# A hybrid encoder layer on one core: query products behind the value evictions, the first head's attention three products later, five buffers for high halves and 51 ring tiles

## The chip, the core and the metric

The kernel runs on one core of a Trainium2 chip. Five engines work side by side, each on its own queue of instructions: TensorE (PE: matmuls and, as PEld, the loads of their weights), VectorE (DVE), ScalarE (ACT), GpSimd (POOL) and SyncE (SP, which here only issues DMAs). The metric is the device time of one execution in microseconds (us); lower is better. Before the change three runs took 2608.44, 2610.34 and 2613.16 us, so the median is 2610.34 us.

## What is computed

One encoder layer, in fp32, over 2048 prompt tokens and 64 tokens of a second sequence with a state. The input projection makes ten groups of 1024 columns. Path A is a gated convolution of width 3. Path B is a chunked recurrence with 8 heads of 128 columns: each head needs a query `q`, a forget gate `f`, a value `iv` and an output gate `zB`.

```python
h = rms_norm(x, g_pre)
proj = jnp.einsum('btd,dn->btn', h, w_in)
vA, bA, cA, zA, q, f, iv, zB, gA, gB = split_cols(proj)
fg = lb + (1.0 - lb) * jax.nn.sigmoid(f)
logf = jnp.log(fg); kk = 1.0 - fg
qq = jax.nn.silu(q) * QK_SCALE; vv = iv
...                                   # per chunk of 64 tokens, per head:
b = jnp.cumsum(logf, axis=1)
ref = b[:, (L - 1) // 2][:, None]
qe = q * jnp.exp(b - ref); ke = k * jnp.exp(ref - b)
att = jnp.where(causal, einsum('bthk,bshk->bhts', qe, ke), 0.0)
o = einsum('bhts,bshv->bthv', att, v) + einsum('bthk,bhkv->bthv', q * jnp.exp(b), S)
S_new = jnp.exp(b_last)[..., None] * S + einsum('bshk,bshv->bhkv', k * jnp.exp(b_last[:, None] - b), v)
...
yB = einsum('btc,cd->btd', rms(o) * g_onorm * jax.nn.silu(zB), w_b_out)
merged = jax.nn.sigmoid(gA) * yA + jax.nn.sigmoid(gB) * yB
x = x + rms_norm(einsum('btd,de->bte', merged, w_o), g_post)
gate = jax.nn.sigmoid(einsum('btd,de->bte', rms_norm(x, g_ple), w_ple_gate))
x = x + einsum('btp,pd->btd', p, w_ple_proj) * gate
```

## The kernel before

**Tiles and blocks.** The 2112 tokens (the 64 stand inside the prompt, at a cut) are worked in 3 blocks of 704, each in two halves of 352 columns. Every fp32 operand is split into a high part `hi` (a cast, on ACT) and a low part `lo` (a subtraction, on DVE), and a product of two operands is three matmuls: hi·hi (L363), hi·lo (L364), lo·hi (L365). A weight tile is 128x512 (256 KB): SP loads it into a `raw` buffer (L198), ACT casts it to `hi` (L188, or L218 once the low part exists), and in block 0 DVE subtracts the low part (L188) and SP stores it as `low`. In blocks 1 and 2 SP loads the stored low part back (L219), into a buffer `lo` or `s`.

**Groups of seven products.** `sgroup` (L349) computes two column groups for both halves with seven products in place of eight, from sums of weight blocks (S1 to S4, made in block 0 by DVE at L297 and stored) and sums of operands (T1 to T4). A product is 12 matmuls of 128x352 into one PSUM bank; there are 5 banks for these (`pg`) and 3 for the attention (`pa`). The products go to the banks a, c, d, b, a, c, d. ACT copies the banks of the first three (L377), DVE adds the fourth (L383), and the last three are evicted by a function `sink` that the caller gives, through `into` (L407 on ACT, L409 on DVE) and `whole` (L402). With `by_k` the first four products advance together, k by k.

**Path B of a block.** `path_b` (L1014 to L1032) goes over the heads. `head_prep` (L826) runs one group for F and Q and one for ZB and IV. After the third product of the second group its inner function `scaled` is called (as `mid`): three exponentials and a Silu on ACT (L855 to L859), then on DVE the scaled keys `ka` and `kb` (L874 to L879), the product of neighbouring chunk factors (L880, on 128x5), the scaled queries `qe` (L881) and `qx` (L882). `sink_v` (L884) evicts the values into `vt` and the gate into `z`. `head_attn` (L896) is a generator in four steps for each part of the block (one of four 128-token tiles and shorter ones): transposes and scores (L929 to L952), state updates (L958, L975), output and its mean square (L994 to L1003), the transpose back (L1008) and the gate (L1010). The steps lie in a list `hooks`; after each product one is taken from it, so that the attention of one head runs between the products of the next. For the first head of block 0 three empty entries are put ahead (L1026).

**Around it.** Each block runs gates (`gates`), path B, path A, the merge of both (block 0: `merge`, then blocks 1 and 2: `in_turn` with L496 to L498), the output projection and the last gate (L529 to L531). A tile scheduler decides the final order on each engine: it follows the order of the program and priorities (`high_priority`, `issue_after`, `behind_all`), and gives a tile that is written a slot of its pool as soon as the slot's last use lets it. On each engine instructions start in that order, so what stands behind a waiting one waits too.

**Pools that the change touches.** Tiles `r` come from a ring of `RING` slots of 708 fp32 per partition (L40). The weight pool has 5 slots for `raw`, 4 for `hi`, 4 for `lo` and 3 for `s`. POOL issues loads into `r` slots: the spilled gates and outputs (L1081), the next block's columns of x (L643), the weights for the sums of the next stage (L320).

Of the kernel before, what the change touches and what calls it, by code (L numbers as in the profile page):

```python
# [11 lines left out]
F32R = mybir.dt.float32r  # L12
# [6 lines left out]
P = 128  # L19
# [17 lines left out]
BN = 704  # L37
HN = BN // 2
NB = TOK // BN
RING = 52  # L40
HALVES = 9

LEAD = 7
# [39 lines left out]
def hybrid_step(  # L83
# [22 lines left out]
    wp = ctx.enter_context(tc.tile_pool(name="wp", bufs=4))  # L106
# [8 lines left out]
    def nm(s):  # L115
        uid[0] += 1
        return f"{s}_{uid[0]}"
# [94 lines left out]

    def split_w(raw, key=None, queue=SP):

        hi = wp.tile([P, 4, P], F32R, tag="hi", name=nm("hi"))
        if key in lows:
            lo = low_tile()
            A.copy(hi, raw)  # L218
            SP.dma_start(lo.bitcast(F32), lows[key])  # L219
            return hi, lo  # L220
        lo = wp.tile([P, 4, P], F32R, tag="lo", name=nm("lo"))
        split(raw, hi, lo)
        if key is not None:
            lows[key] = dram.tile([P, 4, P], F32, tag=f"lo{key}", name=nm("low"), bufs=1)
            queue.dma_start(lows[key], lo.bitcast(F32))
        return hi, lo
# [12 lines left out]
    last, hooks, copies, adds = [None], [], [None], [None]  # L239
# [154 lines left out]
    def half(t, h):  # L394
        return t[:, h * HN : (h + 1) * HN]
# [9 lines left out]
    def into(dst, x, y):  # L405
        if y is None:
            A.copy(dst, x)  # L407
        else:
            V.tensor_tensor(dst, x, y, ALU.add)  # L409
# [413 lines left out]
    def chunks(t):  # L823
        return t.rearrange("p (c t) -> p c t", t=CH)

    def head_prep(bl, hc, hd, first, hs):  # L826
        n, npair = bl["n"], bl["npair"]
        nch, np1 = n // CH, npair * P
        sf, qe = rt(), rt()

        def sink_f(c, h, x, y):
            if c == 0:
                A.activation(half(sf, h), whole(x, y), AF.Sigmoid)
            else:
                into(half(qe, h), x, y)

        if hs and hd == 0:
            plain_group(FF * 8, QQ * 8, hs, sink_f)
        else:
            sgroup(FF * 8 + hd, QQ * 8 + hd, hc, sink_f, first)  # L840
        lg, b, eq = rt(), rt(), rt()
        A.activation(lg, sf, AF.Ln, bias=lb[:, hd : hd + 1], scale=omlb[:, hd : hd + 1])
        A.activation(sf, sf, AF.Identity, bias=omlb[:, hd : hd + 1], scale=nomlb[:, hd : hd + 1])
        V.tensor_tensor_scan(b, keep[:, :n], lg, 0.0, ALU.mult, ALU.add)
        ref = chunks(b)[:, :, CH // 2 - 1 : CH // 2]
        V.tensor_tensor(chunks(lg), chunks(b), ref.to_broadcast([P, nch, CH]), ALU.subtract)
        qc = small.tile([P, 2, BN // CH], F32, tag="qc", name=nm("qc"))
        f, r = qc[:, 0, :nch], qc[:, 1, :nch]
        ka, kb, qx, vt, z = hf(HN + 32), rt(), rt(), rt(), rt()

        def scaled(after):


            with tc.issue_after(after):
                A.activation(r, ref.rearrange("p c o -> p (c o)"), AF.Exp)  # L855
                A.activation(eq, lg, AF.Exp)
                exps = A.activation(lg, lg, AF.Exp, scale=-1.0).ins
            with tc.issue_after(exps):
                A.activation(qe, qe, AF.Silu)  # L859
            V.tensor_tensor(f[:, 1:nch], r[:, 1:nch], chunks(eq)[:, : nch - 1, CH - 1], ALU.mult)  # L860
            V.tensor_copy(f[:, 0:1], r[:, 0:1])
            for g in bl["groups"]:
                if g["sample"]:
                    c = g["off"] // CH
                    V.tensor_copy(f[:, c : c + 1], r[:, c : c + 1])
            f1, f2 = f[:, 0 : 2 * npair : 2], f[:, 1 : 2 * npair : 2]
            ka3 = ka[:, : (nch + 1) // 2 * CH].rearrange("p (g t) -> p g t", t=CH)
            two = kb[:, : 4 * P].rearrange("p (c q t) -> p c q t", q=4, t=CH)
            rest = kb[:, 4 * P : np1].rearrange("p (g c t) -> p g c t", c=2, t=CH)[:, :, 0, :]

            def pairs(x, at):
                return x[:, : 4 * P].rearrange("p (c e h t) -> p c e h t", e=2, h=2, t=CH)[:, :, :, at, :]

            V.tensor_tensor(ka3, chunks(sf)[:, 0:nch:2, :], chunks(lg)[:, 0:nch:2, :], ALU.mult)  # L874
            V.tensor_tensor(two[:, :, 1:3, :], pairs(sf, 1), pairs(lg, 1), ALU.mult)
            V.tensor_tensor(kb[:, 4 * P :], sf[:, 4 * P :], lg[:, 4 * P :], ALU.mult)
            by = f2[:, :4].rearrange("p (c e) -> p c e", e=2).unsqueeze(3).to_broadcast([P, 2, 2, CH])
            V.tensor_tensor(two[:, :, 0:4:3, :], ka3[:, :4, :].rearrange("p (c e) t -> p c e t", e=2), by, ALU.mult)
            V.tensor_tensor(rest, ka3[:, 4:npair, :], f2[:, 4:npair].unsqueeze(2).to_broadcast([P, npair - 4, CH]), ALU.mult)  # L879
            V.tensor_tensor(f2, f2, f1, ALU.mult)  # L880
            V.scalar_tensor_tensor(qe, qe, QK_SCALE, eq, ALU.mult, ALU.mult)  # L881
            V.tensor_tensor(chunks(qx), chunks(qe), f.unsqueeze(2).to_broadcast([P, nch, CH]), ALU.mult)  # L882

        def sink_v(c, h, x, y):  # L884
            if c == 1:
                into(half(vt, h), x, y)
            else:
                A.activation(half(z, h), whole(x, y), AF.Silu)

        sgroup(ZB * 8 + hd, IV * 8 + hd, hc, sink_v, first, mid=scaled)  # L890
        return dict(eq=eq, f=f, ka=ka, kb=kb, qe=qe, qx=qx, vt=vt, z=z, last=bl["last"], carry=None)

# [120 lines left out]
    def path_b(bl, hc, first, kept, fills, hs):  # L1013


        def keep_z(hd, z):
            kept["o", hd] = spill("o", hd)
            G.dma_start(kept["o", hd], z)

        for hd in range(NH):  # L1020
            d = head_prep(bl, hc, hd, first, hs)
            if not (first and hd == 0):
                next(fills, None)
            assert not hooks
            attn = [head_attn(i, gs, d, hd) for i, gs in enumerate(bl["parts"])]
            hooks.extend([None] * 3 if first and hd == 0 else [])  # L1026
            for step in range(4):
                hooks.extend(partial(next, g) for g in attn)
                if step == 2:
                    hooks.append(None)  # L1030
            hooks.append(partial(keep_z, hd, d["z"]))
# [8 lines left out]
    def ple(bl, ph, kept, held=None, shared=False):  # L1040


        for j in range(KB):
            if held is not None:
                hi, lo = held[j]
            else:
                raw = wp.tile([P, 4, P], F32, tag="raw", name=nm("raw"), bufs=5)[:, :2, :]
                SP.dma_start(raw, w_ple[j])
                with tc.high_priority():
                    hi = wp.tile([P, 4, P], F32R, tag="hi", name=nm("hi"))[:, :2, :]  # L1050
                    lo = low_tile()[:, :2, :]
                    A.copy(hi, raw)
                    SP.dma_start(lo.bitcast(F32), lows["p", j])
            t = rt()
            for s in bl["segs"]:
                pp, c = ps_attn()[:, :HN], cols_of(s)
                for k, (xhi, xlo) in enumerate(ph):
                    T.matmul(pp, hi[:, k, :], xhi[:, c], start=k == 0, stop=False)
                    T.matmul(pp, hi[:, k, :], xlo[:, c], start=False, stop=False)
                    last[0] = T.matmul(pp, lo[:, k, :], xhi[:, c], start=False, stop=k == 1).ins  # L1060
                with tc.high_priority():
                    if shared and j < 4 and s is bl["segs"][1]:
                        V.tensor_copy(t[:, c], pp)
                    else:
                        copied = copies[0] = A.copy(t[:, c], pp).ins
            if bl["last"]:
                kept["p", j] = t
            else:
                kept["p", j] = spill("p", j)
                G.dma_start(kept["p", j], t)  # L1070
                if not shared:
                    lows["p", j] = dram.tile([P, 2, P], F32, tag=f"lop{j}", name=nm("low"), bufs=1)
                    SP.dma_start(lows["p", j], lo.bitcast(F32))
            with behind_all((copied,) if hooks else ()):
                hook()
            yield
# [299 lines left out]
    for bi, bl in enumerate(blocks):  # L1376
        first, kept = bi == 0, kepts[bi]
# [124 lines left out]
```

## Time and profile before

| | |
|---|---|
| runs | 2608.44, 2610.34, 2613.16 us (median 2610.34) |
| profiled execution | 2611.61 us, span 2609.9 us |
| granted TensorE clock | 1.000 |
| PE busy | 2588.6 us, 99% of the span, 16562 matmuls |
| PEld busy | 2572.5 us, 99% |
| DVE busy | 1667.1 us, 64% |
| ACT busy | 1538.9 us, 59% |
| POOL busy | 392.6 us, 15% |
| DMA | 745.99 MB, mean 286 GB/s |

The profiled execution is one run, 1.27 us longer than the median of the others. A row of the timeline gives the start in us, the duration in us, then engine, line, operation, output and inputs with the shape and, where the engine had been idle, for how long and what released it. Successive matmuls overlap in the records: each is shown as about 0.32 us long, and in a steady stretch one starts 0.16 us after the other, so a lost time on PE is read from the distance of starts. "x3" in a row means that it stands for three instructions.

### The profile page before, as it was taken

The page shows a single profiled execution, that of the slowest core. Times are in us where ns is not written, and L with a number is a line of the kernel's source. Part 1 is how long each engine was busy: PE and PEld are TensorE (multiplying, and loading weights), DVE is VectorE, ACT ScalarE, POOL GpSimd, SP SyncE. Part 2 cuts the span into 40 slices and gives each one's busy share as a digit, 9 for nine tenths or more (in the row PEclk, how much of TensorE's full clock was granted, in tenths as well). Part 3 has the DMA queues.
Part 4 walks back from the last instruction along what each step waited for, and adds up shares of the span by engine and source line. Part 5 has one row for each costly group of instructions (what it writes and reads, how often), then busy time and mean ns, then how long its engine had stood idle before and what let it go on. Part 6 is the DMA issues. An engine that isn't in the chain of part 4 may idle for free.

```text
span 2609.9 us, 47443 instructions
## 1 busy us (share of the span) xinstructions
PE 2588.6 (99%) x16562; PEld 2572.5 (99%) x16562; DVE 1667.1 (64%) x3232; ACT 1538.9 (59%) x2940; POOL 392.6 (15%) x722
## 2 busy tenths in 40 slices
PE   8999999999999999999999999999999999999999
PEld 8999999999999999999999999999999999999998
DVE  8778888888766555455545568553455544568756
ACT  6666665554434644677745556466667744555746
POOL 2000000200441212101112211021000101210220
PEclk9999999999999999999999999999999999999999
DMA  7687787898988997777789989599776789999977
GB/s 285 234 275 259 251 285 257 306 318 286 342 292 285 351 320 259 248 231 224 226 288 359 381 311 312 193 359 358 229 230 220 224 256 335 377 321 309 339 256 240
DMA packets 362672, 745.99 MB, mean 286 GB/s; under 512 B 44640, under 2 KB 49280, under 8 KB 362432
## 3 DMA queue, kind: packets, MB, share of 16 engines
q1 hardware_dynamic: 319680, 579.55, 65.4%
q0 software_dynamic: 42464, 163.37, 17.0%
q8 instruction: 130, 2.13, 0.3%
q14 instruction: 110, 0.90, 0.1%
q10 hardware_dynamic: 288, 0.05, 0.0%
HBM read 531.74 MB, written 211.04 MB: 285 GB/s over the span
## 4 chain that ended last, share of the span: by engine, by line
PE 89%; DMA 3%; DVE 2%; issue 2%; ACT 1%; POOL 1%; DVEq 0%; POOLq 0%; ACTq 0%; SPq 0%
PE pg L363 19%; PE pg L365 19%; PE pg L364 19%; PE pg L496 4%; PE pg L497 4%; PE pg L498 4%; PE pg L530 4%; PE pg L531 4%; PE pg L529 4%; PE pa L994 1%; PE pa L958 1%; PE pa L996 1%; PE pa L944 1%; DMA r<-w_blk 1%; DMA raw<-S 1%
## 5 line engine op out<-in xcount | busy, mean ns | idle before, releaser
L363 PE MATMUL pg<-r,hi 128*128 128x352 f32 x3304 | 1092.9, 331 | 4.6 <-DVE r L409 3.1
L364 PE MATMUL pg<-r,hi 128*128 128x352 f32 x3304 | 1067.6, 323 | 0.0
L365 PE MATMUL pg<-r,lo 128*128 128x352 f32 x2356 | 762.1, 323 | 1.2 <-DMA lo<-low 1.2
L218 ACT CAST hi<-raw 128x512 fp32r<-128x512 f32 x720 | 445.0, 620 | 499.8 <-PE pg L364 165.6
L363 PEld LDWEIGHTS pg<-r,hi 128*128 128x128 f32 x3304 | 622.2, 188 | 9.1 <-DVE r L409 3.2
L364 PEld LDWEIGHTS pg<-r,hi 128*128 128x128 f32 x3304 | 622.2, 188 | 0.0
L365 PEld LDWEIGHTS pg<-r,lo 128*128 128x128 f32 x2356 | 442.3, 188 | 1.8 <-DMA lo<-low 1.7
L365 PE MATMUL pg<-r,s 128*128 128x352 f32 x948 | 306.2, 323 | 0.1
L530 PE MATMUL pg<-r,hi 128*128 128x352 f32 x768 | 248.4, 324 | 0.0
L529 PE MATMUL pg<-r,hi 128*128 128x352 f32 x768 | 248.1, 323 | 0.0
L188 ACT CAST hi<-raw 128x512 fp32r<-128x512 f32 x218 | 134.6, 621 | 153.1 <-PE pg L364 53.5
L188 DVE TENSOR_TENSOR r<-r,r 128x352 fp32r<-128x352 f32 (+3 forms) x298 | 182.8, 637 | 62.7 <-ACT r L188 61.7
L497 PE MATMUL pg<-r,hi 128*128 128x352 f32 x672 | 217.3, 325 | 0.0
L496 PE MATMUL pg<-r,hi 128*128 128x352 f32 x672 | 213.6, 325 | 0.1
L531 PE MATMUL pg<-r,lo 128*128 128x352 f32 x656 | 211.9, 323 | 0.1
L188 ACT CAST r<-r 128x352 fp32r<-128x352 f32 (+3 forms) x298 | 162.2, 580 | 56.9 <-DVE r L1114 15.4
L188 DVE TENSOR_TENSOR lo<-raw,hi 128x512 fp32r<-128x512 f32 x218 | 149.4, 687 | 63.5 <-ACT hi L188 55.2
L365 PEld LDWEIGHTS pg<-r,s 128*128 128x128 f32 x948 | 178.4, 188 | 0.4 <-DMA s<-low 0.4
L188 ACT CAST hi<-s 128x512 fp32r<-128x512 f32 x160 | 98.5, 621 | 123.0 <-PE pg L364 105.8
L377 ACT COPY hf<-pg 128x352 f32<-128x352 f32 x354 | 157.1, 446 | 11.5 <-PE pg L365 10.9
L530 PEld LDWEIGHTS pg<-r,hi 128*128 128x128 f32 x768 | 144.3, 188 | 0.3 <-DVE r L188 0.2
L529 PEld LDWEIGHTS pg<-r,hi 128*128 128x128 f32 x768 | 144.2, 188 | 0.0
(367 smaller groups left out, 4157.0 us busy)
## 6 DMA issues: line engine op xcount, KB each, us to landing
raw<-w_blk SPq DMA_DIRECT2D x570, 256.0 KB, 4.2
lo<-low SPq DMA_DIRECT2D x411, 256.0 KB, 4.4
raw<-S SPq DMA_DIRECT2D x408, 256.0 KB, 4.4
low<-lo SPq DMA_DIRECT2D x314, 256.0 KB, 3.7
s<-low SPq DMA_DIRECT2D x309, 256.0 KB, 4.2
S<-s SPq DMA_DIRECT2D x152, 256.0 KB, 3.2
r<-w_blk POOLq DMA_DIRECT2D x64, 256.0 KB, 7.3
S<-r POOLq DMA_DIRECT2D x64, 256.0 KB, 5.8
```

The lines of the kernel that those rows point to most:

```text
L188: return A.copy(hi, src).ins, V.tensor_tensor(lo, src, hi.bitcast(F32), ALU.subtract).ins
L218: A.copy(hi, raw)
L363: add(hi[:, k, :], xhi, start=start and k == 0, stop=False)
L364: add(hi[:, k, :], xlo, start=False, stop=False)
L365: last[0] = add(lo[:, k, :], xhi, start=False, stop=k == KH - 1).ins
L377: copied = A.copy(got[n], ps[bank])
L496: add(hi[:, k, :], xhi, start=start and k == 0, stop=False)
L497: add(hi[:, k, :], xlo, start=False, stop=False)
L498: last[0] = add(lo[:, k, :], xhi, start=False, stop=k == KH - 1).ins
L529: T.matmul(ps, hi[:, k % 4, :], xhi[:, c], start=k == ks[0], stop=False)
L530: T.matmul(ps, hi[:, k % 4, :], xlo[:, c], start=False, stop=False)
L531: last[0] = T.matmul(ps, lo[:, k % 4, :], xhi[:, c], start=False, stop=k == ks[-1]).ins
```

## The change

Four edits. The product of chunk factors, `qe` and `qx` leave the function `scaled` and become a function `queries`, which is called when the second half of the values has been evicted. For the first head of block 0 six empty entries stand ahead of the attention in place of three. The tag `hi` gets 5 slots in place of 4 (each 512 fp32 per partition). The ring gets 51 slots in place of 52. No instruction is added or left out.

```diff
-RING = 52
+RING = 51
...
     def split_w(raw, key=None, queue=SP):
-        hi = wp.tile([P, 4, P], F32R, tag="hi", name=nm("hi"))
+        hi = wp.tile([P, 4, P], F32R, tag="hi", name=nm("hi"), bufs=5)
...
             V.tensor_tensor(rest, ka3[:, 4:npair, :], f2[:, 4:npair].unsqueeze(2).to_broadcast([P, npair - 4, CH]), ALU.mult)
+
+        def queries():
+            f1, f2 = f[:, 0 : 2 * npair : 2], f[:, 1 : 2 * npair : 2]
             V.tensor_tensor(f2, f2, f1, ALU.mult)
             V.scalar_tensor_tensor(qe, qe, QK_SCALE, eq, ALU.mult, ALU.mult)
             V.tensor_tensor(chunks(qx), chunks(qe), f.unsqueeze(2).to_broadcast([P, nch, CH]), ALU.mult)
...
         def sink_v(c, h, x, y):
             if c == 1:
                 into(half(vt, h), x, y)
+                if h == 1:
+                    queries()
...
-            hooks.extend([None] * 3 if first and hd == 0 else [])
+            hooks.extend([None] * 6 if first and hd == 0 else [])
```

Line numbers behind the edit are larger by 3 (L880 becomes L883) and, from `sink_v` on, by 5 (L1001 becomes L1006). The order on the engines moves at these places.

On DVE, in the third head of block 0 (the other heads of block 0 from the third on read alike): `r_1802` is `qe`, `r_2061` is `qx`, `r_2062` is `vt`, `pg_2155` the bank of the sixth product. Before:

```order
L880 TENSOR_TENSOR qc_2058<-qc_2058 128x5
L881 SCALAR_TENSOR_TENSOR r_1802<-r_1802,r_2053 128x704
L188 TENSOR_TENSOR lo_2310<-s_2305,hi_2309 128x512
L297 TENSOR_TENSOR s_2337<-raw_2287,s_2315 128x512
L297 TENSOR_TENSOR s_2470<-raw_2456,raw_2458 128x512
L188 TENSOR_TENSOR lo_2320<-s_2315,hi_2319 128x512
L882 TENSOR_TENSOR r_2061<-r_1802,qc_2058 128x704
L297 TENSOR_TENSOR s_2480<-raw_2458,raw_2460 128x512
L188 TENSOR_TENSOR lo_2326<-raw_2287,hi_2325 128x512
L1010 SCALAR_TENSOR_TENSOR r_1385<-pa_2241,vec,r_1385 128x128
L409 TENSOR_TENSOR r_2062<-hf_2143,pg_2155 128x352
L409 TENSOR_TENSOR r_2062<-hf_2143,hf_2168 128x352
```

and with the change:

```order
L1015 SCALAR_TENSOR_TENSOR r_1354<-pa_2238,vec,r_1354 128x128
L297 TENSOR_TENSOR s_2470<-raw_2456,raw_2458 128x512
L409 TENSOR_TENSOR r_2062<-hf_2143,pg_2155 128x352
L188 TENSOR_TENSOR lo_2320<-s_2315,hi_2319 128x512
L409 TENSOR_TENSOR r_2062<-hf_2143,hf_2168 128x352
L297 TENSOR_TENSOR s_2480<-raw_2458,raw_2460 128x512
L883 TENSOR_TENSOR qc_2058<-qc_2058 128x5
L884 SCALAR_TENSOR_TENSOR r_1802<-r_1802,r_2053 128x704
L188 TENSOR_TENSOR lo_2326<-raw_2287,hi_2325 128x512
L885 TENSOR_TENSOR r_2061<-r_1802,qc_2058 128x704
L188 TENSOR_TENSOR lo_2332<-raw_2285,hi_2331 128x512
L1015 SCALAR_TENSOR_TENSOR r_1354<-pa_2259,vec,r_1354 128x64
```

The two evictions of the values (L409) now stand ahead of the three query operations, and the eviction of the bank also stands ahead of one subtraction and one weight sum.

On DVE, in the second head of block 0, where the first head's attention runs: `ms_1530` (before) and `ms_1572` (with the change) is the mean square of the part of four tiles, and L1003, now L1008, scales that part's output, which the transposes on PE read. Before:

```order
L880 TENSOR_TENSOR qc_1380<-qc_1380 128x5
L881 SCALAR_TENSOR_TENSOR r_1149<-r_1149,r_1375 128x704
L188 TENSOR_TENSOR lo_1629<-raw_1620,hi_1628 128x512
L882 TENSOR_TENSOR r_1383<-r_1149,qc_1380 128x704
L188 TENSOR_TENSOR lo_1639<-s_1634,hi_1638 128x512
L1001 TENSOR_REDUCE ms_1530<-r_1529 128x4
L297 TENSOR_TENSOR s_1676<-raw_1626,s_1654 128x512
L591 TENSOR_SCALAR ms_1530<-ms_1530 128x4
L1001 TENSOR_REDUCE ms_1554<-one_1553 128x1
L1001 TENSOR_REDUCE ms_1576<-lone_96 64x1
L188 TENSOR_TENSOR lo_1649<-s_1644,hi_1648 128x512
L1003 TENSOR_TENSOR r_1529<-pa_1521,ms_1530 128x512
```

and with the change:

```order
L883 TENSOR_TENSOR qc_1349<-qc_1349 128x5
L884 SCALAR_TENSOR_TENSOR r_1149<-r_1149,r_1344 128x704
L188 TENSOR_TENSOR lo_1644<-s_1639,hi_1643 128x512
L885 TENSOR_TENSOR r_1352<-r_1149,qc_1349 128x704
L297 TENSOR_TENSOR s_1827<-raw_1805,raw_1807 128x512
L188 TENSOR_TENSOR lo_1650<-raw_1611,hi_1649 128x512
L1006 TENSOR_REDUCE ms_1572<-r_1571 128x4
L402 TENSOR_TENSOR hf_1590<-hf_1434,pg_1472 128x352
L591 TENSOR_SCALAR ms_1572<-ms_1572 128x4
L1006 TENSOR_REDUCE ms_1597<-one_1596 128x1
L1006 TENSOR_REDUCE ms_1689<-lone_96 64x1
L1008 TENSOR_TENSOR r_1571<-pa_1563,ms_1572 128x512
```

The same row of operations stands later against the head's products: between the scaled keys (L874) and the first mean square there are now also five state additions and a copy, two evictions, three subtractions and three weight sums.

On SP, in block 1, where stored low parts are loaded: `lo_11580` is the tile that its product needs next. Before:

```order
L198 DMA raw_11577<-S_1072_4256 128x512
L219 DMA s_11574<-low_4252 128x512
L198 DMA raw_11583<-S_1077_4266 128x512
L219 DMA lo_11580<-low_4262 128x512
L198 DMA raw_11589<-S_1082_4276 128x512
L219 DMA s_11586<-low_4272 128x512
```

and with the change:

```order
L198 DMA raw_11583<-S_1077_4266 128x512
L219 DMA s_11574<-low_4252 128x512
L198 DMA raw_11589<-S_1082_4276 128x512
L219 DMA lo_11580<-low_4262 128x512
L198 DMA raw_11595<-w_blk 128x512
L219 DMA s_11586<-low_4272 128x512
```

Each load of a raw tile now stands one place further ahead of the loads of low parts; so it is throughout blocks 1 and 2.

More of the change, by code (lines that the diff above doesn't have):

```diff
@@ L865, in scaled @@
                     V.tensor_copy(f[:, c : c + 1], r[:, c : c + 1])
-            f1, f2 = f[:, 0 : 2 * npair : 2], f[:, 1 : 2 * npair : 2]
+            f2 = f[:, 1 : 2 * npair : 2]
             ka3 = ka[:, : (nch + 1) // 2 * CH].rearrange("p (g t) -> p g t", t=CH)
@@ L1049, in ple @@
                 with tc.high_priority():
-                    hi = wp.tile([P, 4, P], F32R, tag="hi", name=nm("hi"))[:, :2, :]
+                    hi = wp.tile([P, 4, P], F32R, tag="hi", name=nm("hi"), bufs=5)[:, :2, :]
                     lo = low_tile()[:, :2, :]
```

## The prediction

> **What bounds the kernel now.** I read the page first, then the waits of PE, then PE's timeline around each place where two of its starts lie far apart.
>
> ```profile
> PE 2588.6 (99%) x16562; PEld 2572.5 (99%) x16562; DVE 1667.1 (64%) x3232; ACT 1538.9 (59%) x2940; POOL 392.6 (15%) x722
> ```
>
> PE is busy for 99% of the span, and the change takes no matmul away. So only the time in which PE waits can be won, and any other engine matters only where it makes PE wait. The waits of PE say how much there is:
>
> ```profile
> PE pa L1058 <- ACT r L188: 6.6, 1, 6.6
> PE pg L363 <- DVE r L409: 3.1, 9, 0.6
> PE pa L1008 <- DVE r L1003: 1.7, 1, 1.7
> PE pg L363 <- ACT hi L218: 1.5, 2, 0.7
> PE pg L365 <- DMA lo<-low: 1.2, 1, 1.2
> ```
>
> The first is the start of the program, which the change does not touch. The next four, 7.5 us in all, are what the four edits can reach. The rows count idle time; I count by starts, since a matmul that follows another starts 0.16 us after it. For L409:
>
> ```profile
> 179.67 0.33 PE L364 MATMUL pg<-r,hi 128*128 128x352 f32 x1
> 179.84 0.32 PE L365 MATMUL pg<-r,lo 128*128 128x352 f32 x1
> 180.40 0.43 PE L363 MATMUL pg<-r,hi 128*128 128x352 f32 x1 [0.25 <-DVE r L409]
>   PE pg L363: 1.5, 6
> ```
>
> The last row is from the view of line L409 between 160 and 440 us: six such waits, one per head from the third of block 0 on. Each shows 0.25 us idle and costs 180.40 - 179.84 - 0.16 = 0.40 us; six cost 2.4 us. The other three of the nine lie in path A, where DVE waits for weights that POOL loads; nothing there moves.
>
> **Queries behind the evictions.** Why is the bank late? The timeline of DVE at the same place:
>
> ```profile
> 174.36 0.89 DVE L881 SCALAR_TENSOR_TENSOR r<-r,r 128x704 f32<-128x704 f32 x1
> 175.16 0.68 DVE L188 TENSOR_TENSOR lo<-s,hi 128x512 fp32r<-128x512 f32 x1
> 175.76 0.69 DVE L297 TENSOR_TENSOR s<-raw,s 128x512 f32<-128x512 f32 x1
> ...
> 179.83 0.51 DVE L409 TENSOR_TENSOR r<-hf,pg 128x352 f32<-128x352 f32 x1
> 405.00:426.00 21.00, 20.75 (x134) 20.39 (x133) 18.77 (x41) 16.45 (x28) 2.14 (x3) 1.00 0.64 208
> ```
>
> DVE works without a gap in this stretch (the last row, from the view by windows, gives the same stretch of the last head: 18.77 of 21.00 us), so L409 starts when what is queued ahead is done. From L881 to the next start it is 0.80 us (L882 works on the same 128x704), from a 128x512 subtraction or sum to the next 0.60. In the new order L880 (0.1), L881, L882, two subtractions and one weight sum no longer stand ahead of the eviction: 0.1 + 2 x 0.80 + 3 x 0.60 = 3.5 us. L409 would start near 176.3 and end 3.2 us before PE wants the bank at 180.00. All six stalls go: **-2.4 us**. What is late next is L402, which frees the last bank of the group; the same operations stand ahead of it as before, and that bank is wanted four products (of 12 matmuls, 1.9 us each) after the one that filled it, so it has the slack. The queries are read by the scores (L943), which come as hooks of the next head's products; that covers their delay. In blocks 1 and 2 DVE is not backed up, and the edit is worth nothing there.
>
> The Trainium skill, in Perfetto Trace Analysis, section Optimization Strategy, says that the same gap repeating on the engine that should be saturated can mean too few buffers for the next tile. By that reading five banks would be the cause, and -2.4 would be 0. The trace bears it out only in part: the bank is short by 0.4 us, but its eviction is held up for longer than that in DVE's queue.
>
> **The first head's attention.** The one wait for L1003:
>
> ```profile
> 123.06 0.32 PE L364 MATMUL pg<-r,hi 128*128 128x352 f32 x1
> 125.08 0.63 PE L1008 MATMUL pa<-ident,r 128*128 128x128 f32 x4 [1.70 <-DVE r L1003]
> 127.00 0.32 PE L365 MATMUL pg<-r,lo 128*128 128x352 f32 x1
> 127.45 0.30 PE L1008 MATMUL pa<-ident,one 128*128 128x128 f32 x1
> 118.10 0.79 ACT L859 ACTIVATE r<-r 128x704 f32<-128x704 f32 x1
> 119.99 0.60 ACT L1000 ACTIVATE r<-pa 128x512 f32<-128x512 f32 x1
> 121.74 0.68 DVE L1001 TENSOR_REDUCE ms<-r 128x4 f32<-128x512 f32 x1
> 122.93 0.16 DVE L591 TENSOR_SCALAR ms<-ms 128x4 f32<-128x4 f32 x1
> 124.25 0.69 DVE L1003 TENSOR_TENSOR r<-pa,ms 128x512 f32<-128x512 f32 x1
> ```
>
> It costs 125.08 - 123.06 - 0.16 = 1.86 us, and the second part's transpose 0.29 more: 2.15 us. The squares (L1000) queue behind the next head's exponentials on ACT, which end with L859. Three products later they fall behind them. But DVE then has more ahead of the mean square. PE would want the transpose 36 matmuls later, at 123.22 + 36 x 0.16 = 129.0. In the new order six 128x512 operations (0.60 each), two evictions (0.5) and six small operations (between the 0.16 of L591 and an eviction; I take 0.3) join those ahead of L1001: 6.4 us, so L1001 moves from 121.74 to 128.1; the eight records of L958 that no longer stand ahead of the third product give back up to 0.9.
>
> ```profile
> 105.73 0.89 PE pa L958 x8
> ```
>
> From there one reduction and one eviction (0.6 + 0.5) lead to L591, and it is 124.94 - 122.93 = 2.0 us more to the end of L1003: 130.3 to 131.2. On the other side attention matmuls that come to lie ahead push PE's wish later by up to the same 0.9, to 129.9. So 0.4 to 2.2 us of the stall may stay, and none if DVE was not full throughout. I take 0.5, near the lower end, because the exponentials and all behind them start earlier than before: 2.15 - 0.5 gives **-1.65 us**.
>
> **A fifth buffer for high halves.** Two waits of 0.74 us (1.5 us in the waits), at the start of the gates of blocks 1 and 2; the first:
>
> ```profile
> 850.04 0.48 PE L363 MATMUL pg<-r,hi 128*128 128x352 f32 x2
> 851.26 0.43 PE L363 MATMUL pg<-r,hi 128*128 128x352 f32 x1 [0.74 <-ACT hi L218]
> 850.24 0.45 ACT L377 COPY hf<-pg 128x352 f32<-128x352 f32 x1 [2.96 <-PE pg L365]
> 850.58 0.62 ACT L218 CAST hi<-raw 128x512 fp32r<-128x512 f32 x1
> ```
>
> The cast waits for a free `hi` slot, though ACT idles 2.96 us. With a fifth slot it runs in that gap, and PE then waits only for the bank's copy (L377), whose end at 850.69 lies 0.51 us before the cast's end at 851.20. Two times 0.51: **-1.0 us**; -1.8 if PE need not wait for the copy, 0 if the weights themselves come late.
>
> The same buffer lets SP load the next raw tile one place further ahead of the low parts, in a stretch where the transfers fill the DMA engines:
>
> ```profile
> 890.00:910.00 20.00, 18.81 (x121) 18.52 (x120) 8.67 (x15) 12.08 (x23) 4.95 (x8) 1.00 1.05 401
> 895.32 0.32 SPq L219 DMA_DIRECT2D lo<-low  x1
> 896.98 0.32 SPq L198 DMA_DIRECT2D raw<-S  x1
> 899.31 0.43 PE L365 MATMUL pg<-r,lo 128*128 128x352 f32 x1 [1.19 <-DMA lo<-low]
> ```
>
> The raw load of 896.98 now precedes the `lo` load that PE waits for. If it is issued no earlier, `lo` is issued 2.0 us later and the stall grows by as much; if a buffer comes free one product (1.93 us) earlier, nothing changes; if the whole queue moves ahead the stall of 1.2 goes. Bounds -1.2 to +2.0; I take 0, since the buffer is what frees the raw slot.
>
> The Trainium skill, in DMA: Bandwidth & Descriptors, section Queues, rings and completion order, says that descriptors of one queue are consumed in ring order. By it the earlier raw load costs the `lo` its own transfer: 256 KB at 401 GB/s is 0.65 us, and the sum would be 0.65 worse. No row here shows two neighbouring loads apart.
>
> **One ring tile less.** Loads into the ring may have to wait for a later release. What waits last (the third row is from the view of the tile `x_fm`):
>
> ```profile
> 830.54 1.07 POOL L643 DMA_DIRECT2D r<-x_fm  x2 [28.38 <-PE pg L531]
> 838.84 0.54 POOL L1191 DMA_DIRECT2D r<-x_fm  x1 [7.23 <-DVE r L188]
> DMA to landing us min/median/max: 3.3/5.5/9.2
> 840.75 0.94 DVE L693 SCALAR_TENSOR_TENSOR r<-r,vec,r 128x704 f32<-128x704 f32 x1
> 845.49 0.53 DVE L188 TENSOR_TENSOR r<-r,r 128x352 fp32r<-128x352 f32 x1 [3.80 <-ACT r L188]
> ```
>
> The last pair of the next block's x is issued at 830.54; DVE has scaled it by 841.7 and then sits idle for 3.8 us because ACT is behind. A delay of up to 3.8 us is covered: 0. The loads ahead of that pair have the 28.38 us of POOL's wait as room.
>
> **Moved by the scheduler.** The merges of blocks 1 and 2 come out in another order of matmuls, on operands that ACT and DVE finish just in time:
>
> ```profile
> 1596.17 0.32 PE L498 MATMUL pg<-r,lo 128*128 128x352 f32 x1
> 1596.58 0.95 PE L496 MATMUL pg<-r,hi 128*128 128x352 f32 x4
> ```
>
> One wait of 0.25 us stands there now. I price one more like it: **+0.25**; at worst five or six of up to 0.6, 3 us; at best none.
>
> **The sum.** -2.4 - 1.65 - 1.0 + 0.25 = -4.8 us. On the profiled execution that is 2611.6 to 2606.8; the median of the runs shown is 1.3 us lower, so I forecast **2605.5 us**.
>
> **The rivals.** (1) More is won: the cast and the `lo` wait vanish and no new wait comes: -2.4 - 2.15 - 1.8 - 1.2 = -7.5, 2602.8. For it: each stall is small against the slack that it gets. Against: the transfers are already full there. (2) The banks stay short: L409 moves, but L402 or the weight sums behind it take over, and the six stalls remain: -2.4, 2607.9. For it: DVE is full in block 0. Against: 3.2 us of slack. (3) Given back in the merges and at the `lo` load: +3.0 - 0.25 + 2.0 on the sum, 2610.3. (4) Slower: the ring. POOL issues in order; if the pair at 830.54 has to wait for the release after its own, that of 838.84, it is issued 8.3 us later, and where it then lands as late as the slowest of its kind, 9.2 in place of 5.5 us, 8.3 + 3.7 - 3.8 = 8.2 us of stall come at each of the two block changes: 16.4 - 4.8 = +11.6, 2621.9. It decides from a delay of 3.8 us on. For it: the pair already waits for its slots. Against it: the release follows matmuls of a loop that frees tiles one after the other.
>
> **How the numbers follow.** Forecast 0.54; (1) 0.15, (2) 0.08, (3) 0.10, (4) 0.13. The measurement tells about 0.2%, 5.2 us, from no change: faster means under 2605.1. The forecast lies at that bound, with single runs 2 us apart either way, so 0.30 of it goes to faster and 0.24 to the same; (1) is faster, (2) and (3) are the same. Faster 0.45, same 0.42, slower 0.13. The range takes in (1), (2) and (3): 2602.0 to 2611.0; the forecast's own is 2603.3 to 2607.5.
>
> **What would show it.** Right: PE's waits for L409 fall from nine to three, L1003's row is gone or below 0.5, those for `hi` fall below 0.4 each. Wrong: L409 or L402 waits still at 179 us and every 48.9 us after; a longer wait for `lo` near 897; new waits of L496 and L497 for L188; waits of L363 near 845 and 1690 that follow late loads of x.

## The result, and the profile after

The changed kernel takes 2607.28 us (median of 20 runs, 2604.07 to 2609.97) against 2611.43 us for the kernel before (20 runs, 2608.44 to 2613.84). The ratio is 0.9984 with a 95% interval of 0.9978 to 0.9991: some 4.2 us less, 0.16%. The forecast was 4.8 us less. The profiled execution took 2607.91 us, 3.7 us less than the one before. Lines behind the edit are larger by 5: L1001 is L1006, L975 is L980, L881 is L884.

First the page, then the longer waits of PE in the changed kernel behind the start of the program (us in total, times, longest):

```profile
span 2606.2 us, 47480 instructions
PE 2584.8 (99%) x16562; PEld 2569.0 (99%) x16562; DVE 1659.5 (64%) x3232; ACT 1532.4 (59%) x2940; POOL 392.3 (15%) x722
```

```profile
PE pg L365 <- DMA lo<-low: 2.0, 3, 1.7
PE pa L999 <- DVE r L980: 1.4, 1, 1.4
PE pa L1063 <- ACT r L1070: 1.3, 2, 0.7
PE pg L529 <- ACT r L188: 1.1, 1, 1.1
PE pg L363 <- DVE r L409: 1.0, 2, 0.6
PE pa L932 <- ACT r L939: 0.7, 1, 0.7
PE pa L620 <- DVE r L639: 0.5, 1, 0.5
PE pg L363 <- ACT hf L377: 0.4, 2, 0.2
```

Three rows of before are gone: L1008 for L1003 (1.7), L363 for the `hi` cast (1.5), and of the nine waits for L409 the six of the heads; the two left are path A's. In their place stand new rows: the output matmul (L999) waits for the state additions (L980), L529 for a split on ACT, and a transpose (L932) for a copy of its bank. The waits for loaded low parts are longer in all (2.0 for 1.2), the longest at another place. By starts, 5.6 us of stalls are gone, net of the shorter waits for L377 that stand where the cast's stood.

But about as much came back as others: with the rows that are not printed here, PE's waits add up to 15.2 us before and to 15.7 after. So these rows do not show where the 3.7 us between the two profiled executions come from. The wait for L1070 at 32 us stands 0.9 us earlier, which is less than two executions of the changed kernel differ there (last section); the rest lies in PE's time outside the rows, and no view here takes that apart. What each edit is worth is therefore read from the times of the single edits below.

The heads, on DVE and then on PE, at the place of the prediction:

```profile
175.38 0.51 DVE L409 TENSOR_TENSOR r<-hf,pg 128x352 f32<-128x352 f32 x1
177.53 0.88 DVE L884 SCALAR_TENSOR_TENSOR r<-r,r 128x704 f32<-128x704 f32 x1
178.93 0.88 DVE L885 TENSOR_TENSOR r<-r,qc 128x704 f32<-128x704 f32 x1
```

```profile
178.67 0.33 PE L365 MATMUL pg<-r,lo 128*128 128x352 f32 x1
178.83 0.32 PE L363 MATMUL pg<-r,hi 128*128 128x352 f32 x1
```

The matmul at 178.83 is the one that waited at 180.40 before. Its bank is free from 175.89 on, 2.9 us ahead (3.2 was forecast), and the query operations run behind.

The start of the second block's gates, on PE and ACT:

```profile
846.04 0.48 PE L363 MATMUL pg<-r,hi 128*128 128x352 f32 x2
846.74 0.43 PE L363 MATMUL pg<-r,hi 128*128 128x352 f32 x1 [0.22 <-ACT hf L377]
846.24 0.45 ACT L377 COPY hf<-pg 128x352 f32<-128x352 f32 x1 [2.98 <-PE pg L365]
```

PE now waits for the copy of the bank alone, as forecast.

The first head's attention, where the new wait stands; PE, then DVE:

```profile
119.45 0.32 PE L363 MATMUL pg<-r,hi 128*128 128x352 f32 x1
121.11 0.71 PE L999 MATMUL pa<-r,att 128*128 128x128 f32 x4 [1.35 <-DVE r L980]
```

```profile
115.08 0.56 DVE L874 TENSOR_TENSOR hf<-r,r 128x384 f32<-128x384 f32 x1 [0.65 <-ACT r L857]
117.33 0.29 DVE L977 COPY r<-pa 128x128 f32<-128x128 f32 x1
118.57 0.34 DVE L980 SCALAR_TENSOR_TENSOR r<-r,qc,pa 128x128 f32<-128x128 f32 x1
120.72 0.34 DVE L980 SCALAR_TENSOR_TENSOR r<-r,qc,pa 128x128 f32<-128x128 f32 x1
```

The state additions of the first head stand behind the second head's scaled keys (L874), and those wait for ACT's exponentials. The last of the three that L999 needs ends at 121.06, 1.5 us after PE wants it (119.45 + 0.16).

### The profile page after: what moved, and what is told of

Same layout as the page of the kernel before. It is cut to its first block, busy times and chain, and to the rows that moved or that the text cites. A ratio compares the mean times of both kernels' runs of the same rounds, so it can differ in the third digit from the quotient of the medians.

```text
span 2606.2 us, 47480 instructions
## 1 busy us (share of the span) xinstructions
PE 2584.8 (99%) x16562; PEld 2569.0 (99%) x16562; DVE 1659.5 (64%) x3232; ACT 1532.4 (59%) x2940; POOL 392.3 (15%) x722
## 5 line engine op out<-in xcount | busy, mean ns | idle before, releaser
L363 PE MATMUL pg<-r,hi 128*128 128x352 f32 x3304 | 1091.6, 331 | 1.5 <-DVE r L409 1.0
L363 PEld LDWEIGHTS pg<-r,hi 128*128 128x128 f32 x3304 | 621.6, 188 | 4.6 <-issue 1.8
L529 PE MATMUL pg<-r,hi 128*128 128x352 f32 x768 | 248.4, 324 | 1.1 <-ACT r L188 1.1
L497 PE MATMUL pg<-r,hi 128*128 128x352 f32 x672 | 217.2, 325 | 0.1
L496 PE MATMUL pg<-r,hi 128*128 128x352 f32 x672 | 213.4, 325 | 0.2 <-ACT r L188 0.2
L531 PE MATMUL pg<-r,lo 128*128 128x352 f32 x656 | 212.0, 323 | 0.0
L377 ACT COPY hf<-pg 128x352 f32<-128x352 f32 x354 | 157.0, 446 | 7.9 <-PE pg L365 7.1
L529 PEld LDWEIGHTS pg<-r,hi 128*128 128x128 f32 x768 | 144.1, 188 | 1.4 <-ACT r L188 1.4
```

Of the source, the lines that this page charges most:

```text
L363: add(hi[:, k, :], xhi, start=start and k == 0, stop=False)
L377: copied = A.copy(got[n], ps[bank])
L496: add(hi[:, k, :], xhi, start=start and k == 0, stop=False)
L497: add(hi[:, k, :], xlo, start=False, stop=False)
L529: T.matmul(ps, hi[:, k % 4, :], xhi[:, c], start=k == ks[0], stop=False)
L531: last[0] = T.matmul(ps, lo[:, k % 4, :], xhi[:, c], start=False, stop=k == ks[-1]).ins
```

## The experiments

Twelve runs, each timed in five rounds beside the kernel before. A ratio is to before, with its 95% interval; waits are read from one profiled execution of each. Diffs are against the changed kernel, with lines left out at the three dots; the tag `hi` is made at a second place, where its edit is the same and is not printed. Where the queries are in their old place, lines behind the edit are larger than before by 1 in place of 5.

**The queries alone.** Hi 4, ring 52 and three entries as before.

```diff
-RING = 51
+RING = 52
...
-tag="hi", name=nm("hi"), bufs=5)
+tag="hi", name=nm("hi"))
...
-[None] * 6 if first and hd == 0
+[None] * 3 if first and hd == 0
```

> The queries behind the evictions alone (hi 4, ring 52, three empty entries). Theory (each edit takes away its own stall and they add up): the six waits of L363 for L409 at 179.8, 228.8 ... 424.5 us go, 2.4 us; the waits for L1003 at 123 (1.7 us idle) and for hi at 850 and 1697 (0.74 each) and lo at 898 stay: about 2.4 us faster than before. Rival (the banks are short, or L402 takes over): waits of 0.2 to 0.3 us return at the same places, within 0.5 us of before.

2607.93 us, ratio 0.9989 (0.9981 to 0.9998), 2.6 to 2.9 us less. All six waits are gone, and none of L402 came. The wait for the first head's output became shorter too (1.70 before):

```profile
123.66 0.52 PE L1013 MATMUL pa<-ident,r 128*128 128x128 f32 x3 [1.17 <-DVE ms L591]
```

The theory holds: five banks are enough here once the eviction is not held up.

**Six entries alone.** The queries in their old place, hi 4, ring 52.

```diff
-RING = 51
+RING = 52
...
-tag="hi", name=nm("hi"), bufs=5)
+tag="hi", name=nm("hi"))
...
-
-        def queries():
-            f1, f2 = f[:, 0 : 2 * npair : 2], f[:, 1 : 2 * npair : 2]
+            f1 = f[:, 0 : 2 * npair : 2]
             V.tensor_tensor(f2, f2, f1, ALU.mult)
...
-                if h == 1:
-                    queries()
```

> Six empty entries alone. Theory: the wait for L1003 (1.86 and 0.29 us by starts) goes, and the wait of the output matmul for the state additions of about 1.5 us, which the changed kernel shows at 119.5, comes in its place: net 0.3 to 0.9 us faster, the six L409 waits stay. Rival (that new wait comes from the queries' place, not from the empty entries): no such wait here and 2.1 us faster.

2610.56 us, ratio 1.0000 (0.9991 to 1.0009). The wait for the state additions is there (1.3 us idle, 1.48 by starts) in place of the 2.15 us. So the new wait comes from the empty entries and not from the queries; what is left of the gain (0.3 to 0.9 us was expected) cannot be told from nothing.

**The fifth buffer with ring 51, alone.** The queries in their old place, three entries.

```diff
-        def queries():
-            f1, f2 = f[:, 0 : 2 * npair : 2], f[:, 1 : 2 * npair : 2]
+            f1 = f[:, 0 : 2 * npair : 2]
             V.tensor_tensor(f2, f2, f1, ALU.mult)
...
-                if h == 1:
-                    queries()
...
-[None] * 6 if first and hd == 0
+[None] * 3 if first and hd == 0
```

> The fifth hi buffer and ring 51 alone. Theory: the two waits for hi fall from 0.74 us to about 0.22 (then for L377), 1.0 us in all; the wait for a lo low part is of about the same size as before, perhaps at another place: 1 us faster, within 1 of that. Rival (raw loads put ahead of the low parts cost more than the buffer wins): waits for lo sum to over 2.2 us and the kernel is not faster than before.

2615.12 us, ratio 1.0019 (1.0010 to 1.0028): 4.6 us slower. The theory said 1 us faster; the rival said not faster, but by waits for low parts. Its waits of PE:

```profile
PE pg L363 <- DVE r L409: 3.2, 7, 0.5
PE pa L1009 <- DVE r L1004: 3.1, 1, 3.1
PE pa L1059 <- ACT r L1066: 1.3, 2, 0.7
PE pg L531 <- DVE lo L188: 1.3, 1, 1.3
PE pg L529 <- ACT r L188: 1.2, 1, 1.2
PE pg L365 <- DMA lo<-low: 1.0, 3, 0.6
PE pg L363 <- ACT hf L377: 0.4, 2, 0.2
```

The cast waits fell as they should (last row), and the waits for loaded low parts did not grow. Most of the loss is in block 0: the wait for the first head's output went from 1.7 to 3.1 us, and the six waits for L409 from 0.40 to 0.65 us each by starts. Of the rest, L531's wait is 1.3 us and L529's 1.2; the next kernel shows that L529's comes without the buffer too. A cast that finds a free buffer can run earlier on ACT, and what follows from it comes earlier into DVE's queue. At 56 us such a cast stands ahead of the very copy that PE waits for. ACT of this kernel, and then of before:

```profile
54.49 0.78 ACT L188 CAST r<-r 128x704 fp32r<-128x704 f32 x1 [0.27 <-DVE r L678]
55.18 0.61 ACT L188 CAST hi<-raw 128x512 fp32r<-128x512 f32 x1
55.70 1.15 ACT L1066 COPY r<-pa 128x352 f32<-128x352 f32 x3
```

```profile
55.29 0.78 ACT L188 CAST r<-r 128x704 fp32r<-128x704 f32 x1 [0.21 <-DVE r L678]
55.98 1.15 ACT L1065 COPY r<-pa 128x352 f32<-128x352 f32 x3
```

That costs 0.5 us of PE, in every profile with the fifth buffer (0.72 or 0.73 us idle at this place) and in none without it (0.25 at most). In the third head of block 0 the order is another too: a subtraction stands ahead of L874 that stood behind it (171.35 against 170.88 in before). Rows of this kernel, then one of before:

```profile
170.41 0.29 DVE L1004 TENSOR_TENSOR lone<-pa,ms 64x128 f32<-64x128 f32 x1 [0.33 <-POOL ms L593]
172.54 0.68 DVE L188 TENSOR_TENSOR lo<-raw,hi 128x512 fp32r<-128x512 f32 x1
173.13 0.55 DVE L874 TENSOR_TENSOR hf<-r,r 128x384 f32<-128x384 f32 x1
182.04 0.51 DVE L409 TENSOR_TENSOR r<-hf,pg 128x352 f32<-128x352 f32 x1
```

```profile
168.21 0.29 DVE L1003 TENSOR_TENSOR lone<-pa,ms 64x128 f32<-64x128 f32 x1 [0.33 <-POOL ms L593]
```

But that subtraction is not what makes L409 late. From the scaling of the shortest part (first row, and the row of before) to L409 it is 11.63 us here and 11.62 in before (179.83), so the 0.25 us are lost ahead of it. That the six waits and the first head's grow with the buffer is shown by this kernel beside the next; by which operations they grow is not shown.

**Ring 51 alone.** Hi 4, the queries in their old place, three entries: the edits of the last kernel, and

```diff
-tag="hi", name=nm("hi"), bufs=5)
+tag="hi", name=nm("hi"))
```

> Ring 51 alone, hi 4. Theory: loads into the ring wait a little longer and PE does not see it: within 0.5 us of before, same waits of PE. Rival (the ring costs): waits of L363 after late loads of x near 845 and 1690, or of L496 and L529 for ACT's splits, and 1 us or more slower.

2610.47 us, ratio 1.0001 (0.9992 to 1.0010). The profiled execution, with 2614.42 us the slowest of its runs, has no wait after late loads of x. Its waits for the first head's output (1.7 us) and for L409 (0.30 to 0.34 us idle each) are near those of before (1.7 and 0.25). Among the new ones is this:

```profile
PE pg L529 <- ACT r L188: 1.2, 1, 1.2
```

So the tile costs nothing that the time tells, within the 2.3 us of the interval, and the loss in block 0 of the kernel above is the buffer's. But L529's wait near 1630 us is the ring's: it stands in all seven profiles with ring 51 (0.25 to 1.24 us) and in none of the seven with ring 52. Some 7 us ahead of it ACT sits idle for a weight tile that is still being loaded, 1.8 to 3.4 us in the profiles with ring 51 and 1.0 to 2.0 in those with ring 52; that this makes the wait is likely, but not shown.

**Queries and six entries, without the buffer.** The changed kernel with hi 4 and ring 52.

```diff
-RING = 51
+RING = 52
...
-tag="hi", name=nm("hi"), bufs=5)
+tag="hi", name=nm("hi"))
```

> Queries behind the evictions and six empty entries, with hi 4 and ring 52. Theory A (the fifth buffer wins its 1.0 us at 846 and 1696 as soon as the queries are moved): 1 us slower than the changed kernel, about 3 us faster than before; waits for hi of 0.74 us are back, those for L409 in block 0 stay gone. Theory B (the fifth buffer costs in every setting, as it did alone, by subtractions that come earlier into DVE's queue): 2 to 5 us faster than the changed kernel.

2606.63 us, ratio 0.9984 (0.9976 to 0.9993): as the changed kernel. Neither theory: with the queries moved the fifth buffer and the tile together neither win nor lose what can be measured. Yet PE's waits add up to 12.1 us here, and to 15.7 and 14.5 in the two profiles of the changed kernel; what makes up for that is not shown.

**The changed kernel with three entries.**

```diff
-[None] * 6 if first and hd == 0
+[None] * 3 if first and hd == 0
```

> The changed kernel with three empty entries instead of six. Theory A (the empty entries cover what the fifth buffer does to the first head's attention): the wait for L1003 (L1008 there) comes back with 2 us or more, and the kernel is 1 to 2 us slower than the changed one. Theory B (the empty entries only trade one wait for another, as alone): within 0.7 us of the changed kernel.

2609.59 us, ratio 0.9993 (0.9984 to 1.0002), 2.3 us above the changed kernel's median, though the intervals meet. The wait that the entries took away is back, and longer than with the queries alone (1.17):

```profile
125.83 0.63 PE L1013 MATMUL pa<-ident,r 128*128 128x128 f32 x4 [1.96 <-DVE r L1008]
```

Theory A fits: with the fifth buffer the entries cover a longer wait.

**The changed kernel with the queries back.** Six entries, hi 5, ring 51.

```diff
-        def queries():
-            f1, f2 = f[:, 0 : 2 * npair : 2], f[:, 1 : 2 * npair : 2]
+            f1 = f[:, 0 : 2 * npair : 2]
             V.tensor_tensor(f2, f2, f1, ALU.mult)
...
-                if h == 1:
-                    queries()
```

> The changed kernel with the queries back in their old place (six entries, hi 5, ring 51). Theory A (the fifth buffer's loss in block 0 is the queries' place: alone the six waits for L409 grew from 0.40 to 0.65 us each): those six waits of 0.65 are there, 3.9 us, and the kernel is about 4 us slower than the changed one. Theory B (the loss lies elsewhere, at 832 and 1636 us): waits for L409 of 0.40 us or less, 2.4 us slower or less.

2613.69 us, ratio 1.0012 (1.0003 to 1.0021), 6.4 us above the changed kernel's median (7 us by the ratios). The six waits for L409 have 0.46 to 0.50 us idle each, 0.61 to 0.66 by starts: 3.8 us. Theory A, with a loss larger than its 4 us: besides these stand a second wait at the first head (0.9 us) and one of L531 (1.0 us).

**Five and four entries, without the buffer.** The version with hi 4, ring 52 and the queries moved, and for the second kernel 4 in place of 5:

```diff
-[None] * 6 if first and hd == 0
+[None] * 5 if first and hd == 0
```

> Queries behind the evictions and five empty entries, hi 4, ring 52. Theory (with six entries the state additions of the first head stand behind the next head's scaled keys on DVE, which wait for ACT's exponentials; with five they stand ahead of them): the wait of the output matmul for the state additions (1.54 us by starts with six) is gone, and no wait for L1003's line over 0.5 us comes in its place: 1.0 to 1.6 us faster than with six, about 5.3 us faster than before. Rival (the wait only changes its place again, as from three to six): one wait of 1 us or more between 115 and 130 us, within 0.7 us of the version with six.

> The same with four empty entries. Theory: the state additions stand ahead too, but the squares come nearer to the exponentials on ACT, as with three: a wait of 0.3 to 1.2 us for the scaled output, between the versions with three and with five. Rival: no wait at all, as fast as with five.

Five: 2605.11 us, ratio 0.9981 (0.9972 to 0.9990), 1.5 us below six entries by the medians, though the intervals meet. No wait is left between 56 and 845 us that is over 0.25 us. All the waits of PE behind the start, in the fastest of its runs:

```profile
PE pg L363 <- ACT hi L218: 1.5, 2, 0.7
PE pa L1063 <- ACT r L1070: 0.9, 2, 0.6
PE pg L363 <- DVE r L409: 0.6, 1, 0.6
PE pg L365 <- DMA s<-low: 0.5, 1, 0.5
PE pa L1065 <- DVE r L188: 0.2, 1, 0.2
```

On DVE the state additions now run ahead of the scaled keys, while DVE would otherwise wait for ACT:

```profile
111.68 1.11 DVE L980 SCALAR_TENSOR_TENSOR r<-r,qc,pa 128x128 f32<-128x128 f32 x3
114.60 0.16 DVE L861 COPY qc<-qc 128x1 f32<-128x1 f32 x1 [1.21 <-ACT qc L855]
116.10 0.56 DVE L874 TENSOR_TENSOR hf<-r,r 128x384 f32<-128x384 f32 x1
```

Four: 2606.72 us, ratio 0.9985 (0.9976 to 0.9994), with one wait of 1.7 us at 129 us, for the output of the shortest part (0.3 to 1.2 was expected). Only with five does neither the state addition nor the scaled output come late in the profile; by time four, five and six cannot be told apart.

**Five entries with the fifth buffer.** The changed kernel with five entries.

> The changed kernel with five empty entries in place of six (hi 5, ring 51). Theory (the fifth buffer wins 1.0 us at the two gate starts and gives it back in waits for L529, low parts and at the start): within 0.7 us of the version with five entries and hi 4, ring 52. Rival (with five entries the buffer's loss in block 0 is covered and its gain is left): 1 us faster than that version.

2606.66 us, ratio 0.9984 (0.9975 to 0.9993), 1.6 us above the version without the buffer, with intervals that meet; the theory said within 0.7. The wait for the additions is gone here too. The two cast waits fell, but waits of L531 (1.3 us), of L529 (1.2, the ring's) and for low parts (1.2) are there. So the rival, 1 us faster, falls: nothing of the buffer's gain is seen in the time.

**The changed kernel and five entries without the buffer, on one chip.**

> The changed kernel once more, on the same chip as the next run. Theory: 0.9984 of before again within its interval, the wait of the output matmul for the state additions of 1.4 us again; waits for low parts again over 1 us, at places that may differ, since they hang on DMA timing.

> Queries behind the evictions and five entries, hi 4, ring 52, once more. Theory (it wins what the changed kernel loses at the state additions and at the buffers' waits): 1.5 to 2.5 us faster than the changed kernel on the same chip. Rival: no difference that can be told, within 1 us.

The changed kernel: 2607.75 us (2605.63 to 2610.75, 11 runs), ratio 0.9990 (0.9981 to 0.9999). Five entries, hi 4, ring 52: 2605.79 us (2603.84 to 2606.47, 11 runs), ratio 0.9980 (0.9971 to 0.9989). All 11 runs of the second lie below the median of the first; the difference is 2.0 us in the medians, as the theory said, though the intervals of the two ratios meet. This version had the lower median both times. Against before its intervals lie below 1 both times; against the changed kernel they meet. The changed kernel's waits in this execution:

```profile
PE pa L999 <- DVE r L980: 1.4, 1, 1.4
PE pa L1063 <- ACT r L1070: 1.4, 2, 0.7
PE pg L365 <- DMA lo<-low: 1.3, 2, 0.7
PE pa L620 <- DVE r L639: 0.8, 1, 0.8
PE pg L365 <- DVE lo L188: 0.6, 1, 0.6
PE pg L531 <- DVE lo L188: 0.5, 1, 0.5
```

Against the first profile of the same kernel, the waits for the additions and for L1070 are the same to 0.1 us. Those for low parts (1.3 for 2.0) and L620 (0.8 for 0.5) changed, and L531's and the one for a subtracted low part are new.

The kernels side by side, ratio to before:

| queries moved | entries | hi, ring | ratio | 95% interval |
|---|---|---|---|---|
| no | 3 | 4, 51 | 1.0001 | 0.9992 to 1.0010 |
| no | 6 | 4, 52 | 1.0000 | 0.9991 to 1.0009 |
| no | 3 | 5, 51 | 1.0019 | 1.0010 to 1.0028 |
| no | 6 | 5, 51 | 1.0012 | 1.0003 to 1.0021 |
| yes | 3 | 4, 52 | 0.9989 | 0.9981 to 0.9998 |
| yes | 6 | 4, 52 | 0.9984 | 0.9976 to 0.9993 |
| yes | 3 | 5, 51 | 0.9993 | 0.9984 to 1.0002 |
| yes | 6 | 5, 51 (the change) | 0.9984 | 0.9978 to 0.9991 |
| yes | 6 | 5, 51 (again) | 0.9990 | 0.9981 to 0.9999 |
| yes | 5 | 4, 52 | 0.9981 | 0.9972 to 0.9990 |
| yes | 5 | 4, 52 (again) | 0.9980 | 0.9971 to 0.9989 |
| yes | 5 | 5, 51 | 0.9984 | 0.9975 to 0.9993 |

## Why the prediction was right, point by point

**The queries: -2.4, measured -2.6 to -2.9 alone, and the mechanism as described.** The eviction has 2.9 us of slack where 3.2 were counted from DVE's rows. Rival (2), that the banks stay short, is out. What the prediction did not see is that with the fifth buffer this edit is worth 6.4 us (2613.69 to 2607.28), since it also takes away what that buffer does to the same six waits (3.8 us of it).

**The first head: -1.65, alone nothing that can be told (ratio 1.0000, within 2.3 us).** The wait named did go. The step that failed is the 0.4 to 2.2 us of the stall that "may stay": it was worked out for the chain through the mean square, and that chain was in time. The additions of the state (L975) were counted there only as work ahead of the mean square; that PE itself waits for them, one matmul earlier in the same chain, was not asked. They cost 1.5 us. With the other edits the six entries were worth about 1.3 us (ratios 0.9989 to 0.9984) and 2.3 us (0.9993 to 0.9984), near the term, with intervals that meet in both cases.

**The fifth buffer: -1.0, and the two waits fell by just that, 0.74 to 0.22 us each.** But the term's net was 0 in the change and +4.6 us alone. The step that failed is that it was priced only where PE had waited for a cast. In block 0, where the prediction itself shows DVE full, an earlier cast changes the order on ACT and DVE. At 56 us the cast goes ahead of PE's copy, for 0.5 us in each profile with the buffer; the six waits and the first head's grew by 2.9 us with the buffer alone, by which operations is not shown. The moved queries took the part at the six waits away again.

**The `lo` load: 0 within -1.2 to +2.0.** The waits for loaded low parts came to 2.0 us and 1.3 us in two profiles of the changed kernel, 1.2 before. The place at 898 us is not the one that grew: the longest was near 1040 in both. The rule of the Trainium skill (DMA: Bandwidth & Descriptors, Queues, rings and completion order) would have cost 0.65 us; the two profiles lie 0.8 and 0.1 above before, on both sides of it, so it is neither borne out nor refuted.

**One ring tile less: 0, and alone nothing that can be told** (ratio 1.0001, within 2.3 us). Rival (4) did not happen: no wait after late loads of x stands near 845 or 1690 in any kernel with ring 51. But the tile is not free in the profiles: L529's wait of 0.25 to 1.24 us near 1630 us comes with ring 51 only. The prediction looked at the loads of x alone.

**The scheduler: +0.25.** The waits of L496 and L497 in the merges were two, of 0.15 and 0.11 us idle, near what was priced. L529's wait is the ring's, as said.

So the sum was right to 0.6 us (4.2 for 4.8) and its first term near its measure, in size and in mechanism. The second and third were 1.65 and 5.6 us too hopeful for the edits alone, and the parts helped each other: the edits alone give -2.6 + 0 + 4.6 = +2.0 us, together they give -4.2. The prediction did not reckon with that, so that the whole came out so near is in part luck. The absolute forecast, 2605.5 us, was 1.8 us low, 1.1 of it because the median of before is 2611.43 with 20 runs and was 2610.34 with three.

What stays open: what in PE's time outside the rows makes up for the new waits of the changed kernel; how one ring tile less makes L529 wait; and why L531 waits 0.5 to 1.3 us near 830 us in some executions with the fifth buffer and not in others of the same kernel. No run has the fifth buffer with ring 52.

## What to carry to other kernels

A buffer more also changes when the instructions that fill it run, and so the order on the engines that work on it: price it where those engines are full, not only where PE waits for it. When a chain is moved behind other work, ask of each link that the bounding engine reads, not only of the last, what it now stands behind. Moving low-urgency work behind the eviction that frees a bank was the one edit that paid in every combination. And when single edits give another sum than the whole, measure the edits in pairs before keeping them: here the version with four buffers and the full ring was no slower.

## What was not expected of the hardware

Two executions of the same program, with a granted clock of 1.0 in both, differed by 1.0 us in a single wait: the one for a low part near 1040 us was 1.72 us in one profile of the changed kernel and 0.68 in the other, and L529's at 1630 us was 1.1 and 0.25. The same wait for L1070 at the start stood at 31.93 us in one and at 33.41 in the other. The waits at the first head and at the start (L980 1.4 and 1.4, L1070 1.3 and 1.4), behind work that stands queued on DVE and ACT, repeated to 0.1 us. But not every wait on an engine did: L620's was 0.5 and 0.8, L531's none and 0.5. A difference of a us between two profiles speaks for an edit only at a wait that repeats.
